# Mixture-of-experts weights on one core: all of the routed experts' low parts subtracted on VectorE, one buffer set for down's parts and the turned tokens, a third set of raw weights

## The chip, the cores and the metric

The kernel runs on one core of a Trainium2 chip. Time is device microseconds (us) of one execution, the median of a few runs. The engines of the core are named as the profile names them: PE (TensorE, matmuls; PEld is its weight load), DVE (VectorE), ACT (ScalarE), POOL (GpSimd) and SP (SyncE, which here issues most of the DMAs). TensorE's weight side is fed with a block of tokens, and the experts' weights stream past it.

## The reference

A decoder layer over 1024 tokens of width 1024: attention and an RWKV-7 recurrence side by side, then a mixture of experts. The change lies in the second half:

```
scores = sigmoid(h @ router_w)              # 64 experts in 8 groups
idx, wts = top 6 experts of a token, from its 4 best groups; wts normalised, times 2.5
routed  = sum over a token's 6 experts e of wts * (silu(h @ gate[e]) * (h @ up[e])) @ down[e]
shared  = (silu(h @ sh_gate) * (h @ sh_up)) @ sh_down
x = x + gate2 * (routed + shared);  out = rms_norm(x, final_g)
```

Every expert has gate and up of 1024 x 256 and down of 256 x 1024 float32, 1 MB each, so that the 64 experts hold 201 MB that each have to be read once.

## The kernel before

Products are made nearly as exact as float32 by splitting each operand into a high part (rounded to fp32r by a copy on ScalarE) and a low part (operand minus high part), and adding three products: high by high, high tokens by low weights, low tokens by high weights (`three`, line 1919). So the weights of each expert have to be split on the chip before TensorE may use them. One expert costs four pieces for gate and up (`split_gu`, line 1848: an ACT copy into `guh` on line 1853 and a DVE subtraction into `gul` on line 1854, each 128 x 1024) and two for down (`split_d`, line 1857: an ACT copy into `wdh` on line 1860 and a POOL subtraction into `wdl` on line 1861).

The router sorts the experts by their number of tokens into ranks. A table of fixed blocks (`BLOCKS`, line 1694) gives each rank its blocks of at most 128 token slots: 84 blocks for 64 experts, 20 experts with two to four blocks and 44 with one. Ranks of several blocks stand between those of one. Eight blocks of the shared expert come first. After about 1284 us of the profiled execution TensorE works on routed blocks alone.

`experts` (line 2018) is one loop over the blocks that is written out in full. All engines follow their instructions in the order written, so this order sets the schedule. In the round of block b stand, in this order:

- `up(b)`: 24 matmuls of 512 columns for gate and up;
- if block b is the first of its expert k (`turnover`, line 2053): three of the four pieces of `split_gu` for the next expert, k + 1;
- `act_t(b-1)`: two transposes of the activations, their high part `ah` (ACT, line 1942) and low part `al` (DVE, line 1944);
- `turn(b+1)`: eight transposes of the next block's gathered tokens `xg`, their high parts `xh` (ACT) and low parts `xl` (DVE, line 1915);
- `down(b-1)`: 12 matmuls into `yd`; every third pair (line 1923, `yd<-wdh,al`) needs `al`;
- `swiglu(b)` (ACT, DVE), then the fourth piece of `split_gu` and `split_d`, both for expert k + 1;
- `result(b-1)`: two DVE instructions `ye` (line 1956) and an indirect DMA from POOL that adds the rows to `d_acc` in DRAM (line 1958);
- at a turnover, `need_w(k+3)`: SP reads the expert's number and issues the DMAs of gate, up and down (`fetch`, line 1836). Also per block a gather of token rows `xg` three blocks ahead and of slots `sl` five blocks ahead, both issued by POOL.

Buffers: two sets of split weights (`sets`, for even and odd experts: gate and up and down, high and low), two raw buffers each of gate, up and down, two sets of turned tokens `xts`. A buffer's next user waits for the last user of its bytes, and nothing else.

Of the kernel before, what the change touches and what calls it, by code (L numbers as in the profile page):

```python
# [37 lines left out]
class Kern:  # L38
# [11 lines left out]
    # ---------------------------------------------------------------- constants  # L50
    def consts(self, ctx):
# [3 lines left out]
        with self.pool(name="cset", bufs=1) as sp, self.pool(name="csetp", bufs=1, space=PSUM) as pp:  # L55
# [60 lines left out]
            # silu of c, and the other derived columns  # L116
# [8 lines left out]
    def columns(self, pp):  # L125
        """the other parameters as columns"""
# [40 lines left out]
    # ---------------------------------------------------------------- DRAM scratch  # L167
# [53 lines left out]
    def ada(self, k):  # L221
        """a block of rows of the columns of shift1 and scale1"""
# [3 lines left out]
    def front(self, hp, load, first):  # L226
# [4 lines left out]
        with self.pool(name="frp", bufs=1, space=PSUM) as pp:  # L231
# [26 lines left out]
            def loads():  # L258
                """the rest of the adaLN columns, where x has been, and the first projection's"""
# [13 lines left out]
            def mods():  # L273
                """shift and scale: the sums over blocks of rows by VectorE, then those over lanes by TensorE"""
# [50 lines left out]
    # ---------------------------------------------------------------- projections, RWKV-7 and attention  # L325
    def phase_a(self, psum):
# [142 lines left out]
        # ---- features of RWKV-7  # L469
# [33 lines left out]
        def mixes():  # L503
            for j in range(15):
# [5 lines left out]
                if kind == "small":  # L510
# [3 lines left out]
                    # log_sigmoid and its running sum  # L514
# [76 lines left out]
        def sums(src):  # L591
            """of a pair's two heads, on all their partitions"""
# [4 lines left out]
        def rstds(w, pl, div, eps, least=None):  # L597
            """(sum / div + eps) ** -0.5 of a pair's two heads from the squares w, in rows of tokens and as wide as w"""
# [14 lines left out]
        def turned(w):  # L613
            """512 columns of them in the features' layout"""
# [7 lines left out]
        def kappa():  # L622
            """the scale of kappa"""
# [14 lines left out]
        def pre():  # L638
            """decay and learning rate"""
# [84 lines left out]
        def tokens(src, dst, p, h, pl, dup=None):  # L724
            """512 tokens of a pair's features -> rows of tokens in DRAM"""
# [59 lines left out]
        def merge():  # L785
            """the upper right block: Z11 X12 Z22"""
# [43 lines left out]
        # ---- the recurrence over chunks  # L830
# [10 lines left out]
        def feeds():  # L841
            """what the chain needs of every chunk: rows of v and the state, of b and k, and the inverse"""
# [24 lines left out]
        def prods():  # L867
            """masked products"""
# [82 lines left out]
        def ynorm():  # L951
            """(y - mean) * rstd of every head, in rows of tokens"""
# [22 lines left out]
        # ---- features of attention  # L975
# [4 lines left out]
        def parts(x, h, dst, p, hi, lo):  # L980
            """both parts of a pair's features to DRAM, by way of h: the leading ones from row hi of each head's, the others from row lo"""
# [85 lines left out]
        # ---- attention: the heads for the first half of the tokens, then for the second  # L1067
        def swap_fox():
# [9 lines left out]
            # leading parts of q (64 rows, two of ones, nothing, less the row's maximum) and of k (64 rows, less the running sum  # L1078
            # in two, nothing, ones), and both parts of q and, the other way round, of k
# [36 lines left out]
        def rowmax():  # L1116
            """the rows' maxima, of the scores' leading parts: they only keep exp in range, and cancel in the quotient"""
# [30 lines left out]
        def exps():  # L1148
            """exp of the turned scores, and the values"""
# [62 lines left out]
        # ---- the other adaLN rows, the output projection and the router  # L1212
# [55 lines left out]
    def weave(streams):  # L1268
        """Emits the steps of several (stream, lead) pairs in the order in which their engines would come to them;
        a stream with a lead is served earlier by so much.  # L1270
        A stream yields, after each step, what it held: (engine, time) pairs, ("DMA", latency), ("at", time),
        ("wait", key) and ("set", key) to follow other streams, ("lock", name) and ("unlock", name) to keep them out, ("~engine", time) for what the stream needn't wait for,
        and ("alloc", (name, buffers)) and ("free", name) around the use of shared buffers."""
# [3 lines left out]
        def take(s, t):  # L1277
            """runs one step of a stream and books its time"""
# [526 lines left out]
    def phase_b(self, pg, close_a4, h2):  # L1805
# [212 lines left out]
        def experts():  # L2018
# [13 lines left out]
            for b in range(NB + 1):  # L2032
# [51 lines left out]
                if b < NB:  # L2084
                    if b > 7:
                        need_t(b + 4)
# [97 lines left out]
```

## Time and profile before

| | us |
|---|---|
| three runs | 2237.56, 2241.24, 2254.24 (median 2241.24) |
| span of the profiled execution, first to last instruction | 2247.9 |
| routed blocks: first matmul of the first to last matmul of the last | 1284 to 2213 |
| weights of the first routed expert requested | 1254.9 |
| weights of the last one requested | 2176.9 (its down) |

For the profiled execution only its span is recorded. It is 6.7 us (0.3%) above the median of the runs, so a difference of time in the trace is set against the median as it stands.

How to read the profile: the page gives busy times and digits for 40 slices of 56.2 us, one digit a tenth, PEclk the granted TensorE clock, DMA the mean busy share of 16 DMA engines. The table of stretches gives the same for any window. A timeline row is start, duration, engine, line, operation, output<-inputs, shape, count, and in brackets how long the engine had been idle and what ended that. The table of waits adds those brackets up.

### The profile page before, as it was taken

To read this page: it belongs to the slowest core of one execution; us is meant where nothing else is said; L and a number is where in the kernel's file an instruction comes from. 1 tells how busy PE (TensorE), PEld (TensorE's weight loads), DVE (VectorE), ACT (ScalarE), POOL (GpSimd) and SP (SyncE) were. 2 spreads that over 40 slices of the span, in tenths; PEclk is the share of its full clock that TensorE was granted. 3 is DMA by queue.
4 is the path that set the end of the run, shared out by engine and by line. 5 is a ranking of instruction groups with operands and counts; after the bars stand their busy time and mean duration, and the time that the engine had idled before them with its cause. 6 is when DMAs were issued, how large, how long until landed. Compare 5 with 4: busy or idle time off the path is not lost. (4 is left out here: it accounts for less than half of the span.)

```text
span 2247.9 us, 28260 instructions
## 1 busy us (share of the span) xinstructions
PE 1916.8 (85%) x9746; PEld 1427.7 (64%) x9746; DVE 1489.7 (66%) x2453; ACT 919.3 (41%) x1402; POOL 1142.1 (51%) x830
## 2 busy tenths in 40 slices
PE   4898869889878888789898899888899999999993
PEld 3676657668666666546677677776666666666662
DVE  7736777583475566464777666777877777777774
ACT  5433433313222233343213344455555555555552
POOL 2222221222353233252466656767777777777773
PEclk7998987888878778789899999999999999999997
DMA  6124444646635277683744788899999999988875
GB/s 254 40 85 99 98 94 109 160 119 180 169 106 167 82 216 127 147 250 95 225 164 134 250 226 275 267 301 304 301 303 296 293 286 290 291 284 266 273 246 172
DMA packets 276770, 452.07 MB, mean 201 GB/s; under 512 B 132693, under 2 KB 202409, under 8 KB 250642
## 3 DMA queue, kind: packets, MB, share of 16 engines
q1 hardware_dynamic: 220578, 369.66, 51.3%
q0 software_dynamic: 24768, 66.75, 13.6%
q10 hardware_dynamic: 31280, 13.83, 2.3%
q8 instruction: 78, 1.28, 0.2%
q14 instruction: 66, 0.54, 0.1%
HBM read 355.27 MB, written 94.90 MB: 200 GB/s over the span
## 5 line engine op out<-in xcount | busy, mean ns | idle before, releaser
L1861 POOL TENSOR_TENSOR wdl<-down,wdh 128x1024 fp32r<-128x1024 f32 x128 | 341.0, 2664 | 124.7 <-ACT wdh L1860 124.4
L1854 DVE TENSOR_TENSOR gul<-gate,guh 128x1024 fp32r<-128x1024 f32 x128 | 295.1, 2306 | 62.3 <-ACT guh L1853 62.1
L366 POOL TENSOR_TENSOR wlo<-wraw,whi 128x1024 fp32r<-128x1024 f32 x30 | 78.5, 2617 | 360.4 <-ACT whi L364 340.6
L1958 POOL DMA_INDIRECT d_acc<-ye,ti x84 | 171.9, 2046 | 78.5 <-DVE gul L1854 23.9
L1923 PE MATMUL yd<-wdh,al 128*128 128x512 f32 (+6 forms) x368 | 130.1, 437 | 84.0 <-DVE al L1944 84.0
L1860 ACT ACTIVATE wdh<-down 128x1024 fp32r<-128x1024 f32 x128 | 128.6, 1052 | 173.3 <-issue 172.6
L1923 PE MATMUL gu<-guh,xh 128*128 128x512 f32 (+6 forms) x736 | 192.6, 405 | 1.6 <-ACT xh L1914 1.6
L1923 PE MATMUL gu<-guh,xl 128*128 128x512 f32 (+6 forms) x736 | 185.8, 394 | 0.1
L1923 PE MATMUL gu<-gul,xh 128*128 128x512 f32 (+6 forms) x736 | 185.3, 394 | 0.0
L1923 PEld LDWEIGHTS gu<-guh,xh 128*128 128x128 f32 (+6 forms) x736 | 129.5, 176 | 54.6 <-issue 5.0
L1854 DVE TENSOR_TENSOR gul<-up,guh 128x1024 fp32r<-128x1024 f32 x128 | 158.1, 1235 | 5.6 <-ACT guh L1853 5.0
L1923 PEld LDWEIGHTS gu<-guh,xl 128*128 128x128 f32 (+6 forms) x736 | 121.9, 166 | 49.2 <-issue 1.0
L1923 PEld LDWEIGHTS gu<-gul,xh 128*128 128x128 f32 (+6 forms) x736 | 122.0, 166 | 47.7
L439 PE MATMUL zp<-hTl,whi 128*128 128x512 f32 x480 | 146.9, 446 | 0.0
L1942 ACT ACTIVATE ah<-g 128x256 fp32r<-128x256 f32 (+5 forms) x92 | 31.3, 340 | 280.1 <-PE g L1940 266.9
L439 PE MATMUL zp<-hTh,wlo 128*128 128x512 f32 x480 | 143.7, 437 | 0.0
L1923 PEld LDWEIGHTS yd<-wdh,al 128*128 128x128 f32 (+6 forms) x368 | 63.5, 182 | 125.0 <-DVE al L1944 104.0
L1853 ACT ACTIVATE guh<-gate 128x1024 fp32r<-128x1024 f32 x128 | 134.0, 1047 | 8.1 <-DMA gate<-in_exp_w_gate_dram 8.1
L1956 DVE SCALAR_TENSOR_TENSOR ye<-yd,sl,g 128x512 f32<-128x512 f32 (+12 forms) x168 | 120.6, 740 | 24.8 <-PE yd L1923 21.4
L439 PE MATMUL zp<-hTh,whi 128*128 128x512 f32 x480 | 136.6, 424 | 0.0
L1853 ACT ACTIVATE guh<-up 128x1024 fp32r<-128x1024 f32 x128 | 134.8, 1053 | 2.0 <-DMA up<-in_exp_w_up_dram 2.0
L1923 PE MATMUL yd<-wdh,ah 128*128 128x512 f32 (+6 forms) x368 | 128.8, 433 | 4.2 <-ACT ah L1942 3.7
(461 smaller groups left out, 4238.3 us busy)
## 6 DMA issues: line engine op xcount, KB each, us to landing
gate<-in_exp_w_gate_dram SPq DMA_DIRECT2D x64, 1024.0 KB
up<-in_exp_w_up_dram SPq DMA_DIRECT2D x64, 1024.0 KB
down<-in_exp_w_down_dram SPq DMA_DIRECT2D x64, 1024.0 KB
mw<-in_ada_w_dram SPq DMA_DIRECT2D x32, 512.0 KB
wraw<-in_w_in_dram SPq DMA_DIRECT2D x30, 512.0 KB
xw<-in_ada_w_dram SPq DMA_DIRECT2D x8, 1024.0 KB
xw<-in_x_dram SPq DMA_DIRECT2D x8, 512.0 KB
fb<-d_fb SPq DMA_DIRECT2D x16, 256.0 KB
```

Source lines behind the costliest of these rows:

```text
L366: (nc.vector if j == 1 else nc.gpsimd).tensor_sub(lo, w, h.bitcast(F32))
L439: nc.tensor.matmul(z, a[:, d, :], b[:, d, hs], start=(n == 0 and d == 0), stop=(n == 2 and d == 7))
L1853: nc.scalar.activation(gh[:, qs, n, :], t[:, qs], AF.Copy)
L1854: nc.vector.tensor_sub(gl[:, qs, n, :], t[:, qs], gh[:, qs, n, :].bitcast(F32))
L1860: nc.scalar.activation(dh[:, j], raw[2][:, j], AF.Copy)
L1861: nc.gpsimd.tensor_sub(dl[:, j], raw[2][:, j], dh[:, j].bitcast(F32))
L1923: nc.tensor.matmul(z, x[:, d, :], w[:, d, cs], start=(m == 0), stop=(m == 3 * n - 1))
L1942: nc.scalar.activation(ah[:, :, 0:n], tp[:, :, 0:n], AF.Copy)
L1956: nc.vector.scalar_tensor_tensor(y[0:n, hs], zs[h][0:n], wt, B["g2"][0:n, hs], op0=OP.mult, op1=OP.mult)
L1958: nc.gpsimd.indirect_dma_start(out=self.d_acc, out_offset=ind(ti), in_=y[0:n], in_offset=None, compute_op=OP.add)
```

## The change

- `split_d` subtracts on DVE instead of POOL. In the routed experts POOL then only issues DMAs. (The shared expert's six pieces, `shared`, are unchanged, three of them still on POOL.)
- Down's parts have one buffer set, `wds`, for all experts instead of one in each of two. `split_d` for expert k therefore no longer stands in the round of the first block of k - 1, but at the end of the round of the first block of k, behind `result(b-1)`; its ACT copies wait until `down(b-1)`, the last use by expert k - 1, is through.
- Turned tokens have one set, `xts`, instead of two.
- Raw weights have three buffers each instead of two. `need_w(k+4)` now requests gate and up of expert k + 4 and down of expert k + 3, in two calls of `fetch`, each with a read of the expert's number of its own. Before the loop three experts are requested (of the third gate and up alone).
- The costs with which the order is planned while the first blocks share the engines with the routing are adapted.

Lines in the changed kernel are 1 to 5 higher (1854 becomes 1857, 1861 becomes 1864, 1944 becomes 1947). The diff, without comment lines and without changed signatures that follow from it:

```
         def weight_set(wp):
-            return [wp.tile([128, 8, 2, FE], F32R, name=f"gu{n}") for n in "hl"] + [
-                wp.tile([128, 2, D], F32R, name=f"wd{n}") for n in "hl"]
+            return [wp.tile([128, 8, 2, FE], F32R, name=f"gu{n}") for n in "hl"]
...
-            sets.append(weight_set(pool("bw0")))
+            wp = pool("bw0")
+            sets.append(weight_set(wp))
+            wds.extend(wp.tile([128, 2, D], F32R, name=f"wd{n}") for n in "hl")
...
-            xts.extend([B["fp"].tile([128, 8, 128], F32R, name=f"x{k}{i}", bufs=1) for k in "hl"] for i in range(2))
+            xts.extend(B["fp"].tile([128, 8, 128], F32R, name=f"x{k}", bufs=1) for k in "hl")
...
-            for n, j, c in (("gate", 8, FE), ("up", 8, FE), ("down", 2, D)):
-                t = B["wp"].tile([128, j, c], F32, name=n, bufs=2)
+            for n, j, c in which:
+                t = B["wp"].tile([128, j, c], F32, name=n, bufs=3)
...
+        GU, DN = (("gate", 8, FE), ("up", 8, FE)), (("down", 2, D),)
...
-        def split_d(raw, k):
-            dh, dl = sets[k % 2][2:]
+        def split_d(raw):
+            dh, dl = wds
             for j in range(2):
-                nc.scalar.activation(dh[:, j], raw[2][:, j], AF.Copy)
-                nc.gpsimd.tensor_sub(dl[:, j], raw[2][:, j], dh[:, j].bitcast(F32))
+                nc.scalar.activation(dh[:, j], raw[0][:, j], AF.Copy)
+                nc.vector.tensor_sub(dl[:, j], raw[0][:, j], dh[:, j].bitcast(F32))
                 yield
...
         def need_w(k):
-            if k < NK:
-                raws[k] = fetch(self.eid[0:1, order[k]:order[k] + 1])
+            for kk, to, which in ((k, raws, GU), (k - 1, rawd, DN)):
+                if 0 < kk < NK:
+                    to[kk] = fetch(self.eid[0:1, order[kk]:order[kk] + 1], which)
...
-            need_w(1)
-            need_w(2)
+            for k in range(1, 4):
+                need_w(k)
...
                 if b < NB:
                     act = swiglu(z, m), m
-                    if turnover:
-                        work.append(split_d(raws[k + 1], k + 1))
-                    pieces(2)
+                    pieces(99)
...
                 if b > 0:
                     result(zs, blocks[b - 1][2], weight_of(b - 1), tis[b - 1])
...
-                pieces(99)
                 if b < NB:
+                    if k and blocks[b - 1][0] != k:
+                        work.append(split_d(rawd[k]))
+                        pieces(99)
                     if b > 7:
                         need_t(b + 4)
                     if turnover:
-                        need_w(k + 3)
+                        need_w(k + 4)
```

How this moves instructions, at three places. First VectorE, in the round of a block that is the first of its expert (`gul` gate and up, `al` the activations, `xl` the tokens, `act` the product in SwiGLU, `ye` the result, `ti` the token numbers of a later block). Before:

```order
L1854 TENSOR_TENSOR gul<-gate,guh 128x4x256
L1854 TENSOR_TENSOR gul<-up,guh 128x4x256
L1854 TENSOR_TENSOR gul<-gate,guh 128x4x256
L1944 TENSOR_TENSOR al<-g,ah 128x256
L1915 TENSOR_TENSOR xl_9133<-tp,xh_9132 128x512 x2
L1934 TENSOR_TENSOR act<-act,gu 128x256
L1854 TENSOR_TENSOR gul<-up,guh 128x4x256
L1956 SCALAR_TENSOR_TENSOR ye<-yd,sl,g_8180 128x512 x2
L1893 CAST ti<-sl 128x1
```

And now:

```order
L1857 TENSOR_TENSOR gul<-gate,guh 128x4x256
L1857 TENSOR_TENSOR gul<-up,guh 128x4x256
L1857 TENSOR_TENSOR gul<-gate,guh 128x4x256
L1947 TENSOR_TENSOR al<-g,ah 128x256
L1918 TENSOR_TENSOR xl<-tp,xh 128x512 x2
L1937 TENSOR_TENSOR act<-act,gu 128x256
L1857 TENSOR_TENSOR gul<-up,guh 128x4x256
L1959 SCALAR_TENSOR_TENSOR ye<-yd,sl,g_8180 128x512 x2
L1864 TENSOR_TENSOR wdl<-down,wdh 128x1024 x2
L1896 CAST ti<-sl 128x1
```

Two subtractions of down have come in behind `ye`, and so ahead of the next round's `gul` and `al`; nothing else has changed places. Second GpSimd, two rounds of first blocks before, and three now:

```order
L1888 DMA sl<-d_slot,d_sidx_9830 96x2
L1861 TENSOR_TENSOR wdl<-down,wdh 128x1024
L1958 DMA d_acc<-ye,ti 1152x1024
L1861 TENSOR_TENSOR wdl<-down,wdh 128x1024
L1898 DMA xg<-d_h_191,ti 96x1024
L1888 DMA sl<-d_slot,d_sidx_9830 128x2
L1861 TENSOR_TENSOR wdl<-down,wdh 128x1024
```

```order
L1901 DMA xg<-d_h_191,ti 64x1024
L1891 DMA sl<-d_slot,d_sidx_9826 64x2
L1961 DMA d_acc<-ye,ti 1152x1024
L1901 DMA xg<-d_h_191,ti 64x1024
L1891 DMA sl<-d_slot,d_sidx_9826 128x2
L1961 DMA d_acc<-ye,ti 1152x1024
L1901 DMA xg<-d_h_191,ti 64x1024
```

The subtractions on both sides of the scatter-add are gone, and three DMA issues a block are left. Third SyncE, the requests of one turnover and the start of the next, before:

```order
L1838 TENSOR_LOAD d_eid
L1838 ISA x2
L1842 ISA
L1842 DMA gate<-in_exp_w_gate_dram 128x2048
L1842 ISA
L1842 DMA up<-in_exp_w_up_dram 128x2048
L1842 ISA
L1842 DMA down<-in_exp_w_down_dram 128x2048
L1838 TENSOR_LOAD d_eid
```

And now:

```order
L1839 TENSOR_LOAD d_eid
L1839 ISA x2
L1843 ISA
L1843 DMA gate<-in_exp_w_gate_dram 128x2048
L1843 ISA
L1843 DMA up<-in_exp_w_up_dram 128x2048
L1839 TENSOR_LOAD d_eid
L1839 ISA x2
L1843 ISA
L1843 DMA down<-in_exp_w_down_dram 128x2048
L1839 TENSOR_LOAD d_eid
```

The down that is requested is now that of the expert before, and its number is read once more. ScalarE's rows keep their order (`wdh` twice behind the fourth `guh` in both), but the two `wdh` now belong to the block's own expert instead of the next.

More of the change, by code (lines that the diff above doesn't have):

```diff
@@ L1845, in fetch @@
             return res
+        GU, DN = (("gate", 8, FE), ("up", 8, FE)), (("down", 2, D),)
         def split_gu(raw, k):
-            gh, gl = sets[k % 2][:2]
+            gh, gl = sets[k % 2]
             for q in range(2):
                 qs = slice(q * 4, q * 4 + 4)
-                for n, t in enumerate(raw[:2]):
+                for n, t in enumerate(raw):
                     nc.scalar.activation(gh[:, qs, n, :], t[:, qs], AF.Copy)
@@ L1899, in rows, with turn @@
             return x
-        def turn(b, x, n, turned=False):
-            xh, xl = xts[b % 2]
+        def turn(x, n, turned=False):
+            xh, xl = xts
             if turned:
@@ L1928, in up @@
             z = B["z"] = B["pp"].tile([128, 512], F32, name="gu")
-            return three(z[0:n], xt, [t.rearrange("p j n f -> p j (n f)") for t in w[:2]], 8, slice(None))
+            return three(z[0:n], xt, [t.rearrange("p j n f -> p j (n f)") for t in w], 8, slice(None))
         def swiglu(z, n):
@@ L1945, in act_t, with down @@
             return ah[:, :, 0:n], al[:, :, 0:n]
-        def down(a, w, n):
+        def down(a, n):
             zs = B["zs"] = [B["pp"].tile([128, 512], F32, name="yd") for _ in range(2)]
             for h in range(2):
-                yield from three(zs[h][0:n], a, w[2:], 2, slice(h * 512, (h + 1) * 512))
+                yield from three(zs[h][0:n], a, wds, 2, slice(h * 512, (h + 1) * 512))
         def result(zs, n, wt, ti):
@@ L2052, in experts @@
                         need_s(b + 5)
-                    turnover = k + 1 < NK and (blocks[b - 1][0] != k if k else b == 6)
-                    if turnover:
+                    turnover = k + 1 < NK + 1 and (blocks[b - 1][0] != k if k else b == 6)
+                    if turnover and k + 1 < NK:
                         work.append(split_gu(raws[k + 1], k + 1))
@@ L2063, in experts @@
                 if b + 1 < NB:
-                    xt = turn(b + 1, xs[b + 1], blocks[b + 1][2], b < 7)
+                    xt = turn(xs[b + 1], blocks[b + 1][2], b < 7)
                     if b < 8:
@@ L2067, in experts @@
                 if act is not None:
-                    for s in down(at, sets[blocks[b - 1][0] % 2], act[1]):
+                    for s in down(at, act[1]):
                         if b < 8:
@@ L2073, in experts @@
                     act = swiglu(z, m), m
-                    if turnover:
-                        work.append(split_d(raws[k + 1], k + 1))
-                    pieces(2)
+                    pieces(99)
                     if b < 8:
@@ L2087, in experts @@
                     if turnover:
-                        need_w(k + 3)
+                        need_w(k + 4)
                     if turnover and b < 8:
-                        yield [("~ACT", 4.0), ("~DVE", 2.8), ("~POOL", 4.6)]
+                        yield [("~ACT", 2.0), ("~DVE", 2.3), ("~POOL", 1.0)]
         def rest():
@@ L2099, in rest @@
                 nc.vector.tensor_copy(ei[:, 1:2], self.os[:, ds(o, 1)])
-                raw = fetch(ei[0:1, 0:1])
+                raw, rawd = fetch(ei[0:1, 0:1], GU), fetch(ei[0:1, 0:1], DN)
                 sl = slots(ei[:, 1:2], 128)
@@ L2103, in rest @@
                 x = rows(ti, 128)
-                g, h = split_gu(raw, 0), split_d(raw, 0)
-                xt = turn(0, x, 128)
+                g, h = split_gu(raw, 0), split_d(rawd)
+                xt = turn(x, 128)
                 for s in (g, h):
@@ L2111, in rest @@
                 at = act_t(swiglu(B["z"], 128), 128)
-                for _ in down(at, sets[0], 128):
+                for _ in down(at, 128):
                     pass
```

10 lines of the change are left out of this document (5 added, 5 removed).

## The prediction

> **What bounds the kernel now.** I began with the page: its slices show where each resource is full.
>
> ```profile
> PE   4898869889878888789898899888899999999993
> POOL 2222221222353233252466656767777777777773
> PEclk7998987888878778789899999999999999999997
> DMA  6124444646635277683744788899999999988875
> ...
> L1861 POOL TENSOR_TENSOR wdl<-down,wdh 128x1024 fp32r<-128x1024 f32 x128 | 341.0, 2664 | 124.7 <-ACT wdh L1860 124.4
> L1854 DVE TENSOR_TENSOR gul<-gate,guh 128x1024 fp32r<-128x1024 f32 x128 | 295.1, 2306 | 62.3 <-ACT guh L1853 62.1
> ...
> L1854 DVE TENSOR_TENSOR gul<-up,guh 128x1024 fp32r<-128x1024 f32 x128 | 158.1, 1235 | 5.6 <-ACT guh L1853 5.0
> ```
>
> From slice 24 on (the routed experts) both PE and DMA stand at 8 to 9 tenths. And one thing is odd: the same subtraction costs 2306 ns for gate and 1235 for up. Next, the table of stretches, from the first routed blocks to where the last weights have landed, with 20 us of a full queue ahead of them:
>
> ```profile
> core 0: us, PE busy (x) PEld busy (x) DVE busy (x) ACT busy (x) POOL busy (x), PEclk, DMA share, GB/s
> 1262.00:1282.00 20.00, 18.28 (x81) 14.91 (x81) 10.51 (x18) 7.60 (x11) 13.01 (x8) 0.95 1.02 388
> 1275.00:1400.00 125.00, 117.78 (x551) 95.05 (x550) 77.31 (x107) 54.16 (x84) 77.43 (x47) 0.97 0.86 261
> 1400.00:1500.00 100.00, 87.36 (x403) 69.17 (x402) 77.70 (x88) 54.40 (x77) 74.85 (x40) 0.96 0.87 278
> 1500.00:1800.00 300.00, 272.19 (x1244) 201.76 (x1243) 228.89 (x276) 163.20 (x234) 224.01 (x125) 0.96 0.96 300
> 1800.00:2000.00 200.00, 180.16 (x828) 122.99 (x825) 156.15 (x183) 112.95 (x163) 159.49 (x83) 0.97 0.91 287
> 2000.00:2182.00 182.00, 165.95 (x757) 111.76 (x758) 132.29 (x170) 95.51 (x141) 140.76 (x75) 0.97 0.86 277
> ```
>
> From 1275 to 2182 are 907 us. PE is busy for 823.4 of them (117.78 + 87.36 + 272.19 + 180.16 + 165.95), idle for 83.6. The clock column loses 3 to 4% more: 31 us. The DMA engines' work, share by length, is 107.5 + 87 + 288 + 182 + 156.5 = 821 us: almost as much as PE's. What ends PE's idle time, and what SP's requests wait for, stands in the two tables of waits for the same stretch:
>
> ```profile
> PE yd L1923 <- DVE al L1944: 82.3, 42, 4.7
> ...
> SPq L1842 <- POOL wdl L1861: 479.5, 62, 8.8
> SPq L1842 <- DVE gul L1854: 273.1, 73, 23.7
> ```
>
> So nearly all of PE's idle time is one wait: `down` stops at its third pair for `al`, 42 times at 2.0 us. And the next weights are requested when POOL or DVE lets a raw buffer go; SP waits for that 750 us. Last, the timeline of one round that splits weights:
>
> ```profile
> 1714.46 2.01 ACT L1860 ACTIVATE wdh<-down 128x1024 fp32r<-128x1024 f32 x2 [2.16 <-issue]
> 1716.38 1.04 ACT L1853 ACTIVATE guh<-gate 128x1024 fp32r<-128x1024 f32 x1
> ...
> 1715.60 2.40 POOL L1861 TENSOR_TENSOR wdl<-down,wdh 128x1024 fp32r<-128x1024 f32 x1 [1.37 <-ACT wdh L1860]
> 1718.17 2.26 POOL L1958 DMA_INDIRECT d_acc<-ye,ti  x1 [0.16 <-issue]
> 1719.97 2.88 POOL L1861 TENSOR_TENSOR wdl<-down,wdh 128x1024 fp32r<-128x1024 f32 x1
> 1723.01 1.74 POOL L1898 DMA_INDIRECT xg<-d_h,ti  x1 [0.16 <-issue]
> ...
> 1712.38 1.27 DVE L1915 TENSOR_TENSOR xl<-tp,xh 128x512 fp32r<-128x512 f32 x2
> ...
> 1713.58 0.40 DVE L1934 TENSOR_TENSOR act<-act,gu 96x256 f32<-96x256 f32 x1
> ...
> 1715.04 1.40 DVE L1956 SCALAR_TENSOR_TENSOR ye<-yd,sl,g 96x512 f32<-96x512 f32 x2
> 1716.36 0.14 DVE L1893 CAST ti<-sl 96x1 int32<-96x1 f32 x1
> 1717.45 1.64 DVE L1854 TENSOR_TENSOR gul<-gate,guh 128x1024 fp32r<-128x1024 f32 x1 [0.95 <-ACT guh L1853]
> 1719.01 1.21 DVE L1854 TENSOR_TENSOR gul<-up,guh 128x1024 fp32r<-128x1024 f32 x1
> 1720.15 3.79 DVE L1854 TENSOR_TENSOR gul<-gate,guh 128x1024 fp32r<-128x1024 f32 x1
> 1723.86 0.34 DVE L1944 TENSOR_TENSOR al<-g,ah 128x192 fp32r<-128x192 f32 x1
> ...
> 1714.44 2.03 PE L1923 MATMUL gu<-guh,xh 128*128 128x512 f32 x8
> ...
> 1724.26 0.70 PE L1923 MATMUL yd<-wdh,al 128*96 128x512 f32 x2 [1.73 <-DVE al L1944]
> ...
> 1726.19 2.01 PE L1923 MATMUL gu<-guh,xh 128*72 128x512 f32 x8
> ```
>
> Here is the odd thing's cause. POOL's second subtraction holds from 1719.97 to 1722.85; DVE's `gul`, issued at 1720.15, ends 1.09 later, at 1723.94. The 1.64 beside POOL's first one ends 1.09 after that as well. The two engines' subtractions take turns. `al` stands behind them, PE waits 1.73, and the round takes 11.75 (1714.44 to 1726.19). Undisturbed rows, and a round that splits nothing:
>
> ```profile
> 1958.01 1.22 DVE L1854 TENSOR_TENSOR gul<-gate,guh 128x1024 fp32r<-128x1024 f32 x1
> 1958.45 2.25 POOL L1958 DMA_INDIRECT d_acc<-ye,ti  x1 [1.19 <-DVE ti L1893]
> 1959.14 1.22 DVE L1854 TENSOR_TENSOR gul<-up,guh 128x1024 fp32r<-128x1024 f32 x1
> 1960.28 1.22 DVE L1854 TENSOR_TENSOR gul<-gate,guh 128x1024 fp32r<-128x1024 f32 x1
> ...
> 1957.08 2.00 PE L1923 MATMUL gu<-guh,xh 128*72 128x512 f32 x8
> ...
> 1966.73 0.63 PE L1923 MATMUL gu<-guh,xh 128*72 128x512 f32 x2
> ```
>
> A subtraction costs DVE 1.14 from start to start, also beside a scatter-add issued by POOL. A round without a stall takes PE 9.65.
>
> **The change, part by part.** *Down's low part on DVE.* It takes 2664 ns off POOL 128 times and gives DVE 1.14 instead; and `gul` loses its waits. A round that splits then costs DVE six subtractions, 6.84, `al` 0.34, `act` 0.40, `ye` 1.40, `ti` 0.14 and the tokens' two `xl`, 1.27 for 128 tokens: 10.4. Before, it was 1.64 + 1.21 + 3.79 + 1.21 for `gul` alone, and 11.4 in all. A round that splits nothing costs DVE 3.55. For 64 and 20 of them: 666 + 71 = 737, against PE's 84 x 9.65 = 811: DVE isn't the bound on average.
>
> *Where the stall goes.* Laid out with the rows of the round at 1714: `wdh` 1714.46 to 1716.47, `ye` to 1716.36, then `wdl` twice to 1718.64, `gul` three times to 1722.06. `al` starts there instead of at 1723.86, and PE is ready for it at 1722.53 (1724.26 - 1.73). The stall is gone with 0.4 to spare. What is late next: rounds that split come about three in a row (64 in 84). Each takes DVE 0.75 more than PE's 9.65, so the stalls are about 0, 0.35 and 0.75 there, and 0.75 more with a fourth; a round without splitting clears the debt. With 20 groups that leaves 22 to 37 us. PE's limit from 1284 to 2213 is then 811 + 22 to 37 against 929 now: a gain of 81 to 96. The half-clock stretches, which follow the stalls, are in it.
>
> *Transfers.* They must go 8% faster for that, and have 821 us of work in 907. The most that the trace shows over 300 us is 0.96, with requests still waiting for buffers; with a full queue it is 1.02 (first row of the table). A third raw buffer keeps three experts requested. I take 0.98, in between: 821 / 0.98 = 838, and 4 us more since the first 125 us, with four blocks on one expert, cannot be filled entirely: 842, a gain of 65. At 1.02 it would be 98, at 0.95 39. At 0.98 it is smaller than PE's, so the transfers decide, and the third buffer is worth what lies between 0.96 (859, a gain of 48) and 0.98: about 17 us (none, if 0.96 is the most; 50 at 1.02).
>
> *One buffer set for down.* `wdh` now waits for the `down` just ahead of it. But it did so before: at 1714.46 it began together with the next `up` (1714.44), as `down` ended, since the set of two experts back was in use until then too. ACT's order is the same. The cost is nothing as long as `wdl` is through before the next `down` asks for it, a pair of matmuls before `al`, at about 1722; it is through at 1718.64. PE's `up` and transposes are the cover. Without them copies and subtractions would cost 1718.64 - 1714.46 = 4.2 us a turnover, 267 in all.
>
> *One set of turned tokens.* `xh` waits for the previous `up`; it waited for transposes that stand behind that `up` on PE anyway. Only in the eight shared blocks, which aren't transposed, is it new; there `ah`, ahead of it on ACT, waits for PE's transposes behind `up` too. Nothing; without that cover one `xh` and `xl`, some 2 us, seven times.
>
> *SP's second read of the expert's number.* 64 more; SP waits for buffers 750 of 907 us. Nothing.
>
> The sum: 65 us off 2241, the profiled span being 6.7 over the median: **2176 us**.
>
> **Rivals.**
> *Transfers give way.* If 0.96 is a queue that waits, and not work, PE's limit decides: 81 to 96 off, 2152. For it speaks the 388 GB/s row; against it that 300 GB/s was held for 300 us while requests were outstanding. The Trainium skill (DMA: Bandwidth & Descriptors, Bandwidth) gives HBM about 358 GB/s for a core; the 258 MB that the table's rows add up to would then need an estimated 721 us, and PE would decide. The trace's 388 GB/s over 20 us is above that figure, so I don't sum with it.
>
> *VectorE takes the stall over.* If small gaps between instructions add 0.4 to each round, DVE's 10.4 becomes 10.8, and if the slack of the plain rounds isn't used (`al` is needed in each round, and split weights can be only one expert ahead), a splitting round takes 11.0 to 11.5: 64 x 11.0 to 11.5 + 20 x 9.65 = 897 to 929 against 929, 0 to 32 off: 2225 in the middle. For it: six subtractions in a row now stand ahead of `al`. Against: the laid-out round above has 0.4 to spare.
>
> *Slower: GpSimd's DMA issues take turns with the subtractions* as its own subtractions did. With `d_acc` (2.26) and `xg` (1.74) a block on DVE's bill, DVE needs 737 + 84 x 4.0 = 1073 for 929: 144 slower, 2385. It decides from 2.3 us a block on. Against it: `gul` took 1.22 beside `d_acc` at 1958.45. The Trainium skill (SBUF — State Buffer, Who interferes with whom) says that a VectorE instruction with two SBUF inputs contends with a GpSimd one that reads SBUF, not with one that only writes; the 3.79 and the 1.22 agree.
>
> **How the numbers follow.** Transfers decide, 2176: 0.70, its own range 2143 to 2202 (shares of 1.02 to 0.95). They give way: 0.10. VectorE takes over: 0.13. Slower: 0.07. For 8 in 10 the range takes the first two and most of the third's near side: 2143 to 2216. A measurement tells about 1% (22 us) from no change. Faster by more: 0.70 + 0.10 + a quarter of the third, 0.84; the rest of the third, 0.09, is within 1%; slower 0.07.
>
> **What would show it.** Right: `gul` of gate near 1.22 like up's; PE's waits for `al` under 40 us in all; DMA share 0.97 or more from 1400 to 2050; now and then ACT's `guh` or `wdh` waiting for a landing. Wrong: `gul` or `wdl` over 1.5 (the slower rival); DVE over 0.95 busy with PE still waiting for `al` (VectorE); shares of 0.9 with neither PE nor DVE full, which none of this explains.

## The result, and the profile after

| | before | after |
|---|---|---|
| median of the runs, us | 2247.74 (2237.56 to 2263.71, 4 runs) | 2180.41 (2171.78 to 2194.53, 4 runs) |
| ratio of the times, 95% interval | | 0.9713 (0.9634 to 0.9792) |
| profiled execution: span, us | 2247.9 | 2192.3 (its own time: 2194.53) |
| routed blocks, first matmul to last, us | 1284.2 to 2213.1 = 928.9 | 1298.3 to 2158.8 = 860.5 |

The change saves 67 us where 65 were predicted (2176, range 2143 to 2216). The routed part became 68.4 us shorter. The profiled execution came to that part 14 us later than before. The experiments below, the one with the old front too, came there between 1280 and 1304, so I take this for scatter; it is part of why this execution lies above the median.

The page of the changed kernel, the same lines as before, and the gathers of slots:

```profile
PE   4898888898887789798978889999899998999993
POOL 3322222313433314325256744654556666776652
PEclk7999686888878777799989989999999999999996
DMA  7124354555455365966365498999999999999875
...
L1891 POOL DMA_INDIRECT sl<-d_slot,d_sidx x84 | 198.6, 2364 | 27.5 <-issue 24.4
...
L1857 DVE TENSOR_TENSOR gul<-up,guh 128x1024 fp32r<-128x1024 f32 x128 | 155.5, 1215 | 5.5 <-ACT guh L1856 5.2
...
L1857 DVE TENSOR_TENSOR gul<-gate,guh 128x1024 fp32r<-128x1024 f32 x128 | 155.3, 1214 | 0.0
...
L1864 DVE TENSOR_TENSOR wdl<-down,wdh 128x1024 fp32r<-128x1024 f32 x128 | 150.0, 1210 | 0.1
```

All three kinds of subtraction now take the same 1.21 us; gate's came down from 2306 ns. GpSimd lost 341 us of subtractions, but it is busy for only 169 us less (972.9 after 1142.1), mostly because its DMA issues became longer: `sl` has a mean of 2364 ns, and had 1147 before (102 us more in all), and `xg` takes 31 us more. The stretches of the routed part:

```profile
1275.00:1400.00 125.00, 123.24 (x573) 100.14 (x574) 85.13 (x127) 55.01 (x83) 56.47 (x38) 0.98 0.92 305
1400.00:1500.00 100.00, 97.78 (x465) 76.82 (x463) 83.08 (x114) 60.17 (x85) 61.22 (x29) 1.00 0.96 310
1500.00:1800.00 300.00, 275.52 (x1282) 202.19 (x1282) 237.16 (x331) 173.36 (x247) 175.63 (x85) 0.98 0.96 311
1800.00:2000.00 200.00, 192.67 (x917) 132.19 (x916) 165.44 (x235) 119.55 (x176) 135.28 (x62) 1.00 0.95 316
2000.00:2115.00 115.00, 114.28 (x546) 79.12 (x545) 100.09 (x144) 72.12 (x107) 81.46 (x36) 1.00 0.95 318
```

The last three columns say most: the clock hardly falls any more (stretches at half the clock cost 8.5 us of the routed part, and 32.4 before, worked out from the trace), and the transfers run at 305 to 318 GB/s where they ran at 261 to 300, at a share that is no higher from 1500 to 1800 (0.96) and 0.04 to 0.09 higher elsewhere. TensorE is nearly full in all rows but the third, from 1500 to 1800. What the engines waited for from 1275 to 2160:

```profile
DVE ti L1896 <- DMA sl<-d_slot,d_sidx: 56.3, 34, 4.3
...
DVE ye L1959 <- DMA d_acc<-ye,ti: 41.0, 18, 5.6
...
PE yd L1926 <- DVE al L1947: 25.1, 23, 2.4
...
PE tp L1915 <- DMA xg<-d_h,ti: 10.4, 9, 2.1
```

TensorE's wait for `al` fell from 82.3 to 25.1. Three waits are new (of `xg` there was one before, 1.2), and all three are for GpSimd's small transfers (slots, sums, tokens). None is for weights. Last, the timeline of VectorE and GpSimd in a round that splits weights:

```profile
1575.17 1.40 DVE L1959 SCALAR_TENSOR_TENSOR ye<-yd,sl,g 88x512 f32<-88x512 f32 x2
...
1576.42 6.77 POOL L1891 DMA_INDIRECT sl<-d_slot,d_sidx  x1 [0.30 <-issue]
1576.49 2.35 DVE L1864 TENSOR_TENSOR wdl<-down,wdh 128x1024 fp32r<-128x1024 f32 x2
...
1578.83 1.20 DVE L1857 TENSOR_TENSOR gul<-gate,guh 128x1024 fp32r<-128x1024 f32 x1
...
1579.96 1.21 DVE L1857 TENSOR_TENSOR gul<-up,guh 128x1024 fp32r<-128x1024 f32 x1
...
1581.09 1.21 DVE L1857 TENSOR_TENSOR gul<-gate,guh 128x1024 fp32r<-128x1024 f32 x1
...
1582.58 0.38 DVE L1947 TENSOR_TENSOR al<-g,ah 128x216 fp32r<-128x216 f32 x1 [0.28 <-ACT ah L1945]
```

This is the round that the prediction laid out: `ye`, `wdl` twice, `gul` three times, then `al`, which here waits for `ah` and not for a subtraction. Beside it GpSimd's gather, issued at 1576.42, holds until 1583.19, past the whole run of subtractions, which themselves take their 1.21 (2.35 for two, 1.14 from start to start).

### The profile page after: what moved, and what is told of

It is laid out like the page before. It is cut to its first block, busy times and chain, and to the rows that moved or that the text cites. A ratio compares the mean times of both kernels' runs of the same rounds, so it can differ in the third digit from the quotient of the medians.

```text
span 2192.3 us, 28289 instructions
## 1 busy us (share of the span) xinstructions
PE 1903.1 (87%) x9746; PEld 1417.6 (65%) x9746; DVE 1494.5 (68%) x2581; ACT 918.9 (42%) x1402; POOL 972.9 (44%) x702
## 5 line engine op out<-in xcount | busy, mean ns | idle before, releaser
L1961 POOL DMA_INDIRECT d_acc<-ye,ti x84 | 176.9, 2106 | 282.2 <-issue 65.1
L1891 POOL DMA_INDIRECT sl<-d_slot,d_sidx x84 | 198.6, 2364 | 27.5 <-issue 24.4
L1863 ACT ACTIVATE wdh<-down 128x1024 fp32r<-128x1024 f32 x128 | 128.6, 1052 | 95.6 <-PE yd L1926 91.9
L1901 POOL DMA_INDIRECT xg<-d_h,ti x84 | 150.3, 1789 | 25.8 <-issue 20.9
L1926 PEld LDWEIGHTS gu<-guh,xh 128*128 128x128 f32 (+6 forms) x736 | 125.0, 170 | 50.8 <-ACT xh L1917 1.8
L1857 DVE TENSOR_TENSOR gul<-gate,guh 128x1024 fp32r<-128x1024 f32 x128 | 155.3, 1214 | 0.0
L1864 DVE TENSOR_TENSOR wdl<-down,wdh 128x1024 fp32r<-128x1024 f32 x128 | 150.0, 1210 | 0.1
L1926 PE MATMUL yd<-wdh,al 128*128 128x512 f32 (+6 forms) x368 | 121.2, 411 | 25.6 <-DVE al L1947 25.1
```

Of the source, the lines that this page charges most:

```text
L1857: nc.vector.tensor_sub(gl[:, qs, n, :], t[:, qs], gh[:, qs, n, :].bitcast(F32))
L1863: nc.scalar.activation(dh[:, j], raw[0][:, j], AF.Copy)
L1864: nc.vector.tensor_sub(dl[:, j], raw[0][:, j], dh[:, j].bitcast(F32))
L1891: nc.gpsimd.indirect_dma_start(out=sl[0:n], out_offset=None, in_=self.d_slot, in_offset=ind(idx[0:n]))
L1901: nc.gpsimd.indirect_dma_start(out=x[0:n], out_offset=None, in_=self.d_h2, in_offset=ind(ti))
L1926: nc.tensor.matmul(z, x[:, d, :], w[:, d, cs], start=(m == 0), stop=(m == 3 * n - 1))
```

## The experiments

Theory A is the prediction's: the two engines' subtractions took turns, and with that gone transfers set the first half of the routed part and TensorE the second. Theory B has the gain in the earlier requests of the third raw set, Theory C says that GpSimd's late DMAs cost what is still waited for. D to I come up with the later experiments and are told in their expectations.

The first four share one set of runs of the kernel before (2243.22 us), the next four a second (2245.99), then three (2247.62) and one (2249.57).

**Where the gain is from: e1_dve_only.** The kernel before with this edit alone (two raw sets, two sets of down's parts and of turned tokens):

```
-                nc.gpsimd.tensor_sub(dl[:, j], raw[2][:, j], dh[:, j].bitcast(F32))
+                nc.vector.tensor_sub(dl[:, j], raw[2][:, j], dh[:, j].bitcast(F32))
```

> The kernel before, with one instruction moved: down's low part is subtracted on VectorE, at the old place, with two sets of split weights, two of turned tokens and two raw buffers. Theory A (the gain comes from the subtractions of two engines no longer taking turns): most of the 67 us, so 2180 to 2205, and gate's `gul` at about 1.22 us like up's. Theory B (the gain comes from earlier requests, by the third raw set): 2225 to 2250, within 1% of before.

Measured: 2189.51 us, 0.9758 (0.9698 to 0.9818): 54 us of the gain, by the moved subtraction alone, in Theory A's range; Theory B falls. The 9 us to the changed kernel are within the two intervals.

**The third raw set: e2_two_raw.** The changed kernel with two raw sets:

```
-                t = B["wp"].tile([128, j, c], F32, name=n, bufs=3)
+                t = B["wp"].tile([128, j, c], F32, name=n, bufs=2)
...
-            for k in range(1, 4):
+            for k in range(1, 3):
...
-                        need_w(k + 4)
+                        need_w(k + 3)
```

> The changed kernel with two raw buffers instead of three (requests one expert later). Theory A: 0 to 20 us slower than the changed kernel, 2180 to 2200; by the prediction's estimate 17. Theory B: at least half of the gain is lost, 2215 or more.

Measured: 2182.04 us, 0.9733 (0.9664 to 0.9802). The third set is worth nothing that can be measured.

**Taking turns: e3_pool_again.** The changed kernel with the old place of down's subtraction:

```
-                nc.vector.tensor_sub(dl[:, j], raw[0][:, j], dh[:, j].bitcast(F32))
+                nc.gpsimd.tensor_sub(dl[:, j], raw[0][:, j], dh[:, j].bitcast(F32))
```

> The changed kernel with down's low part back on GpSimd; one set of down's parts, one of turned tokens and three raw sets stay. Theory A: no faster than before, 2240 to 2340, since POOL's two subtractions of 2.7 us now begin only when down of the expert before is through, and hold up the three `gul` and `al` behind them; gate's `gul` back at 2.3 us or more on average. Theory B: 2180 to 2205.

Measured: 2400.85 us, 1.0703 (1.0636 to 1.0770), 220 us over the changed kernel, and above Theory A's range too. Its groups of subtractions, from the page:

```profile
L1857 DVE TENSOR_TENSOR gul<-gate,guh 128x1024 fp32r<-128x1024 f32 x128 | 373.5, 2918 | 76.9 <-ACT guh L1856 76.9
L1864 POOL TENSOR_TENSOR wdl<-down,wdh 128x1024 fp32r<-128x1024 f32 x128 | 337.5, 2926 | 0.0
```

Gate's is lengthened from 1214 to 2918 ns by nothing but the other engine's subtraction; GpSimd's own takes 2926, and took 2664 in the kernel before. So the lengthening is the place of `wdl`, as the prediction read it, and neither buffers nor order cure it. It is worse than the kernel before by 158 us. In the new order `wdl` stands right ahead of the next round's `gul`; that more of them meet there fits the 2918 against 2306, but was not tried by itself.

**The late slots: e4_slots_early.** After the change VectorE waits 56.3 us for slots. Here they are gathered seven blocks ahead:

```
-            sl = B["fp"].tile([128, 2], F32, name="sl", bufs=8)
+            sl = B["fp"].tile([128, 2], F32, name="sl", bufs=12)
...
-                        need_s(b + 5)
+                        need_s(b + 7)
```

> The changed kernel with the slots' gathers issued two rounds earlier (seven blocks ahead instead of five, 12 buffers instead of 8), so that the token numbers on VectorE find them landed. Theory C (what is left of TensorE's waits comes from GpSimd's DMA issues, which in the changed kernel's trace take up to 6.8 us behind a run of subtractions, so that `ti` waits 56 us): 10 to 30 us faster than the changed kernel, 2150 to 2170, and `ti` waits under 10 us. Theory A (the transfers decide in the first half of the blocks and TensorE in the second): within 10 us of the changed kernel, with the same DMA share of 0.95 or 0.96 from 1500 to 1760.

Measured: 2177.94 us, 0.9710 (0.9651 to 0.9769): no change, though `ti` no longer waits; Theory C falls. Its waits show the next one in line:

```profile
DVE ye L1959 <- DMA d_acc<-ye,ti: 65.3, 26, 7.6
```

This was 41.0: the wait moved from the slots to the sums. A table of VectorE's waits alone would have promised 56 us.

**Do transfers decide: e5_half_down and e6_more_loads.** Both are e2 with other loads, in `fetch`; half of down (both halves of its split then read the half that is loaded):

```
+                src = A["exp_w_" + n][0][ds(e, 1)].rearrange("e r c -> (e r) c").rearrange("(p j) c -> p j c", j=j)
+                o = 1 if n == "down" else j
+                nc.sync.dma_start(t[:, 0:o], src[:, 0:o])
```

and half of gate once more, which nothing reads:

```
+                if n == "up":
+                    g = B["wp"].tile([128, 4, FE], F32, name="more", bufs=2)
+                    nc.sync.dma_start(g, A["exp_w_gate"][0][ds(e, 1)].rearrange("e r c -> (e r) c").rearrange(
+                        "(p j) c -> p j c", j=j)[:, 0:4])
```

> The kernel with two raw sets (e2_two_raw, 2182 us) in which only the first half of each expert's down weights is loaded, and both halves of the subtraction read it; it leaves out half of down's weights, 64 x 0.52 MB = 33.5 MB, which at the 311 GB/s of the stretch 1500 to 1800 and its share 0.96 is an estimated 103 us of transfer time at a full share. Theory D (transfers set the pace while 24 of the 90 routed rounds take 10.9 us each, and TensorE's own 9.7 us a round sets it afterwards): the rounds of blocks 28 to 52 fall from 256-262 us to TensorE's 233 to 240, blocks 8 to 28 gain up to 10, and the rest nothing, so 2145 to 2165 us. Theory E (VectorE's queue and GpSimd's held DMA issues set the pace of these rounds as well, and the share of 0.97 is only what they leave): unchanged within 10 us, 2172 to 2192.

> The kernel with two raw sets (2182 us) with an additional load of 0.52 MB an expert into a tile that nothing reads, 33.5 MB in all, an estimated 103 us of transfer time at the rate of the stretch 1500 to 1800. Theory D: the rounds that transfers already set (about 24 of 90) take their whole share of it, some 27 us, and the later ones, which had 3 to 10% of the transfer engines' time left, most of the rest: 2225 to 2275 us, with a DMA share near 0.97 to the end of the routed part. Theory E: the DMA engines have room, and the time rises by less than 15 us, 2172 to 2197.

Measured: e5 2159.08 us, 0.9634 (0.9566 to 0.9702), 23 less than e2 (the intervals overlap a little, at 0.966 to 0.970; the routed parts are 840.1 and 853.6); e6 2221.55 us, 0.9897 (0.9813 to 0.9982), 40 more (routed part 891.2). Theory E falls: loads set part of the time. But 103 us of transfers were worth only 23 and 40, and e6 is under Theory D's range. Its stretches tell why:

```profile
1500.00:1800.00 300.00, 261.36 (x1192) 190.39 (x1192) 222.12 (x307) 157.60 (x226) 154.79 (x80) 0.96 1.00 332
1800.00:2000.00 200.00, 186.58 (x866) 127.95 (x865) 158.00 (x223) 115.52 (x168) 118.37 (x56) 0.97 0.98 332
2000.00:2115.00 115.00, 114.23 (x541) 77.98 (x540) 96.35 (x138) 69.56 (x102) 76.83 (x36) 1.00 1.03 359
```

The same engines carry 332 to 359 GB/s when more is asked of them, where 311 went at a share of 0.96. So 0.96 was no ceiling. Nor is a packet's time fixed: in the queue of SP's loads a MB took the 16 engines 2.78 us before, 2.71 after and in e6 (1500 to 1800), and 2.61 in e6 from 2000 to 2115 (that queue's share times the length, over its MB).

How transfers then decide is in the chain of waits from 1500 to 2100 (shares of these 600 us; "d_acc" is the scatter-add, until it has landed). With half of down:

```profile
by line: PE gu L1927 32.7%; PE yd L1927 17.4%; DMA d_acc<-ye,ti 15.4%; issue 8.9%; PE tp L1916 5.8%; DMA sl<-d_slot,d_sidx 4.8%; DMA xg<-d_h,ti 4.3%; DVE gul L1858 3.4%; POOL sl L1892 2.8%; PE g L1944 1.1%; DVE ye L1960 0.6%; DVE xl L1919 0
```

With more loads:

```profile
by line: DMA d_acc<-ye,ti 33.1%; issue 15.4%; PE gu L1930 13.1%; DMA sl<-d_slot,d_sidx 11.1%; PE yd L1930 8.6%; DVE gul L1861 6.5%; POOL sl L1895 2.8%; PE tp L1919 2.0%; POOL xg L1905 1.5%; DVE ye L1963 1.4%; DVE wdl L1868 1.1%; DVE xl L192
```

With fewer loads the chain runs through TensorE's matmuls (33 + 17%), with more through the small transfers (33 + 11%). The weights come in time either way (with more loads ACT waits 3.1 us for them in all); the small transfers beside them come late.

**The order on VectorE: e7_two_pieces and e9_four_pieces.** The changed kernel with one piece of the split less, or more, at the head of a round:

```
-                    pieces(3)
+                    pieces(2)
```

> The changed kernel with two pieces of the weight split at the head of a round instead of three: the third of the 1.21 us subtractions then stands behind VectorE's copies for the running block, so that al comes about 1.2 us earlier on VectorE and the run of subtractions ahead of it, in which GpSimd's DMA issues are held up to 6.77 us, is shorter. Theory E: TensorE's waits for al (25.1 us) go and held issues get shorter, so 5 to 20 us less than the changed kernel, 2160 to 2175. Theory D: the waits for al fall too, but the time stays within 8 us of the changed kernel's 2180.

Measured: 2210.15 us, 0.9854 (0.9784 to 0.9925): 30 slower than the changed kernel. In the profiled executions 17 us of it lie in the routed part (877.5 after 860.5); the rest is not explained here. Both theories missed it, and the reason for the experiment was wrong in itself: `al` did come sooner, but what waited instead was this (TensorE, 1300 to 2160):

```profile
PE tp L1915 <- DMA xg<-d_h,ti: 31.0, 11, 5.7
PE yd L1926 <- DVE al L1947: 11.9, 19, 1.4
```

The subtraction taken from ahead of `al` now stands ahead of `ye`. The scatter-add needs `ye`, and later blocks' gathers stand behind the scatter-add in GpSimd's queue. The reverse, `pieces(4)`, was to test that:

> The reverse of e7_two_pieces: all four pieces of the next expert's split stand at the head of the round, so that four 1.21 us subtractions run ahead of al, and nothing but act stands between al and ye. Theory F (what the order decides is when ye is ready, since GpSimd's scatter-add waits for it, and the gathers of later blocks stand behind that scatter-add in GpSimd's queue; e7 put a subtraction ahead of ye and lost 30 us): ye comes earlier, so the time is that of the changed kernel or up to 15 us less, 2165 to 2182, although al comes 1.2 us later. Theory E (the run of subtractions ahead of al, in which GpSimd is held, decides): a longer run, so 10 to 30 us more, 2190 to 2210, with more of TensorE's waits for al and more than 40 DMA issues of over 2.9 us.

Measured: 2188.91 us, 0.9766 (0.9698 to 0.9834), 8.5 over the changed kernel: within the intervals, and between the two theories' ranges. The held issues are gone, which Theory E had not expected at all (GpSimd, 1300 to 2115):

```profile
L1901 POOL DMA_INDIRECT xg<-d_h,ti x80 | 98.6, 1233 | 26.3 <-issue 21.8 <-PE yd L1926 3.0 <-PE tp L1915 0.9
L1891 POOL DMA_INDIRECT sl<-d_slot,d_sidx x79 | 85.9, 1087 | 24.1 <-issue 24.1
```

`sl` is at 1087 ns again, 8 issues of all take over 2.9 us where 40 did, and TensorE waits 2.3 us for `xg`. Yet no time is won: `al`, behind four subtractions, made TensorE wait 38.1 us in place of 25.1. So taking the held issues away did not pay for 13 us more of that wait; what they cost by themselves is not shown. That e7 lost its time by the late `ye` fits the 31.0, and e9's 2.3 on the other side; the link by link chain was not shown.

**What holds an issue: e10_memset.** Behind each subtraction an instruction that reads nothing:

```
+                    nc.vector.memset(gap, 0.0)
```

> The changed kernel with a VectorE memset of one column (which reads nothing) behind every fp32 subtraction of the weights: 6 an expert, an estimated 0.06 to 0.1 us each, 0.4 to 0.6 us a round on VectorE. Theory G (a DMA issue of GpSimd is held while VectorE runs instructions with both operands in SBUF back to back, and goes on at the first instruction of another kind): the issues of over 2.9 us (40 in the changed kernel) nearly vanish, and the mean sl issue falls from 2.4 us to under 1.6; if such issues also cost time, 5 to 15 us are won less the memsets, 2168 to 2185. Rival (the issue is held by something else, the semaphores or the queue): sl's issues stay above 2 us, and the time rises by the memsets, 2180 to 2200.

Measured: 2184.39 us, 0.9731 (0.9671 to 0.9792); 35 issues over 2.9 us, `sl` 2.24 us in the mean. Theory G falls, the rival's forecast holds. A gather in this kernel:

```profile
1568.61 6.57 POOL L1895 DMA_INDIRECT sl<-d_slot,d_sidx  x1 [0.30 <-issue]
...
1573.08 1.21 DVE L1858 TENSOR_TENSOR gul<-gate,guh 128x1024 fp32r<-128x1024 f32 x1
1573.09 0.06 DVE L1859 MEMSET gap<- 128x1 f32 x1
...
1574.22 0.37 DVE L1951 TENSOR_TENSOR al<-g,ah 128x216 fp32r<-128x216 f32 x1
```

It ends at 1575.18, 0.96 after `al`, which reads PSUM, begins; 0.99 is the median of a `sl` issue. So it made next to no way during the subtractions, and 0.06 us of another kind between them do not help. Whether they are too short, or run within the neighbour's time, stays open. In the changed kernel's 40 issues of over 2.9 us, the time with no weight subtraction beside them is 0.92 us in the median, worked out from the trace: about a plain gather's time.

But not every issue is held. The changed kernel's trace also has this gather, with the same neighbours as the one at 1576.42:

```profile
1520.47 1.02 POOL L1891 DMA_INDIRECT sl<-d_slot,d_sidx  x1 [0.30 <-issue]
...
1520.54 2.35 DVE L1864 TENSOR_TENSOR wdl<-down,wdh 128x1024 fp32r<-128x1024 f32 x2
```

Of 57 issues that began in a run of subtractions (or at most 0.2 us ahead of it) with 2 us or more of it to come, 32 lasted past its end and 25 ended inside it. In the kernel before, 51 scatter-adds of 54 ended inside. What tells the two kinds apart is not shown.

**More room for the small transfers: e8_room and e11_room_slots.** The changed kernel with two raw sets, slots 7 blocks ahead, tokens 4 ahead in 6 buffers, token numbers a block sooner, 4 buffers for `ye`:

```
-            x = B["fp"].tile([128, D], F32, name="xg", bufs=4)
+            x = B["fp"].tile([128, D], F32, name="xg", bufs=6)
...
-            y = B["fp"].tile([128, D], F32, name="ye")
+            y = B["fp"].tile([128, D], F32, name="ye", bufs=4)
...
-                        need_s(b + 5)
+                        need_s(b + 7)
...
-                        need_t(b + 4)
+                        need_t(b + 5)
```

> A candidate for a better version: the changed kernel with two raw sets, whose room goes to the running gathers and sums: slots gathered 7 blocks ahead (12 buffers), tokens 4 ahead (6 buffers), turned tokens one block earlier, 4 buffers for ye. It takes out all the waits for late GpSimd transfers at once (ti for sl, PE for xg, ye for d_acc), which together ended 108 us of idle time on three engines. Theory E: 10 to 25 us less than the changed kernel, 2155 to 2170. Theory D: those waits move to the weights' landings, which come no earlier, and the time stays within 10 us, 2170 to 2190.

Measured: 2209.38 us, 0.9849 (0.9779 to 0.9919), 29 slower than the changed kernel and outside both theories' ranges; in the profiled executions 15 us of it lie in the routed part (875.2). VectorE's first wait names a buffer that I had not enlarged, that of `ti`:

```profile
DVE ti L1896 <- DMA d_acc<-ye,ti: 75.4, 23, 8.4
```

`ti` cannot be written before the scatter-adds that read its old contents are done. With 12 buffers for it (`name="ti", bufs=12`):

> e8_room with 12 buffers for ti in place of 8. In e8 ti, needed one block earlier, waited 75.4 us for the scatter-adds that still read its 8 buffers, which delayed al (TensorE's waits 42.2 us). Theory H (that wait is all that cost e8 its 29 us over the changed kernel): ti no longer waits, and the time falls to 2160 to 2185. Rival (more gathers ahead are late or harmful for another reason, for example because ye then runs further ahead of its scatter-adds or the gathers take the place of scatter-adds in GpSimd's queue): it stays above 2195.

Measured: 2196.25 us, 0.9796 (0.9739 to 0.9853). 13 of the 29 us are back, a difference within the intervals, and the time is just inside the rival's range (above 2195). In the profiled execution the routed part is 861.7, as long as the changed kernel's 860.5, but this execution, 2186.45, is the shortest of its four. This fits that wait being the routed part's loss, but single executions do not show it, and the rest of the 29 is open. No version here beats the changed kernel.

**Is TensorE the limit: e12_two_terms.** A third of `up` left out in the routed blocks:

```
-                    for s in up(xt, sets[k % 2], m):
+                    for s in up(xt, sets[k % 2], m, 3 if b < 8 else 2):
```

> The changed kernel in which the routed blocks leave out the third of up's three terms (the low part of the tokens times the high part of the weights): 8 of 36 matmuls, about 2.0 us of TensorE's 9.7 us a round; VectorE's work, the loads and the order stay. Theory D (transfers set blocks 28 to 52, TensorE the blocks after): blocks 28 to 52 stay at 255 to 262 us; the others fall until the transfers set them too, which at a share of 0.98 is 809 us in place of 844 for blocks 8 to 91, so at most 35 us less: 2145 to 2170, with a DMA share of 0.96 or more in the last third. Theory I (TensorE's own work sets the pace everywhere, and a share of 0.97 is no limit): 2.0 us less in each of 83 rounds, 166 us, so below 2100. Theory E (the order of VectorE and GpSimd sets it): no change within 10 us, with the DMA share as it was.

Measured: 2168.75 us, 0.9637 (0.9559 to 0.9716): 12 us less than the changed kernel, which its interval does not tell from nothing, for 166 us of TensorE's work. Theory I falls, and Theory E's 10 us are missed by 2. Theory D's range holds, but not its reason, as the time of the routed blocks shows (from first matmul to first matmul, with the DMA share, worked out from the trace; the last weights land before the last stretch ends; the last row is the prediction's 9.65 a round):

| us (share) | blocks 8 to 28 | 28 to 52 | 52 to 72 | 72 to 91 |
|---|---|---|---|---|
| before | 219 (0.86) | 266 (0.96) | 221 (0.92) | 210 (0.81) |
| changed | 196 (0.93) | 263 (0.97) | 201 (0.95) | 185 (0.86) |
| e2, two raw sets | 198 (0.91) | 256 (0.97) | 199 (0.96) | 186 (0.91) |
| e5, fewer loads | 195 (0.87) | 248 (0.93) | 199 (0.92) | 184 (0.83) |
| e6, more loads | 198 (0.94) | 277 (1.00) | 217 (0.98) | 185 (0.99) |
| e12, fewer matmuls | 195 (0.94) | 255 (0.98) | 203 (0.96) | 181 (0.87) |
| TensorE's own 9.65 | 193 | 232 | 193 | 183 |

The changed kernel's first and last stretch run at TensorE's own pace. But with 2 us a round taken from TensorE they keep their time. So another limit lies within a few us of TensorE's there. The trace points at VectorE in the rounds that split: from first matmul to first matmul, e12's take 10.0 us in the first stretch and 9.6 in the last, and VectorE is busy for 9.1 and 9.0 of them. In e12 TensorE waits for `al` again, and VectorE for small transfers (1275 to 2140):

```profile
PE yd L1926 <- DVE al L1947: 92.8, 56, 3.8
...
DVE ti L1896 <- DMA sl<-d_slot,d_sidx: 67.1, 33, 5.7
```

In the middle the loads move the time (248 to 277 in blocks 28 to 52, 199 to 217 in 52 to 72, the latter only upwards), and the matmuls hardly do (255 and 203, beside e2's 256 and 199).

## Why the prediction was right, and where it wasn't

- *Subtractions of two engines take turns.* Shown: gate's `gul` 2306 to 1214 ns, and 2918 with `wdl` back on GpSimd (e3). The prices of 1.14 from start to start and 1.22 for one held for `wdl` too.
- *The stall at `al` goes, and 22 to 37 us come back in runs of split rounds.* TensorE waited 25.1 for `al`, and 10.4 more for `xg`, which the prediction had not named. The table of blocks has 16 experts of several blocks and 48 of one (not 20 and 44, as the description of the kernel has it), so the split rounds come in 16 groups of mostly four, not in 20, and the prediction's own prices give 0.35 + 0.75 + 0.75 for each, 30 in all. In the routed part TensorE's idle time fell by 46.5 us (84.75 to 38.22) and its busy time for the same matmuls by 21.5 (844.25 to 822.78), as the granted clock rose from 0.97 to 0.99: together the 68.
- *Transfers decide, at 821 us of work and a share of 0.98.* The sum 842 was near the 833 measured (1289 to 2122), by two errors against each other; that the whole came out within 2 us is luck. The share from 1400 to 2050 was 0.96, not 0.97 and more. And the work was less than 821: with the 14 us of later start, from 1289 to 2122, the shares add up to an estimated 788 (0.91 x 111 + 0.96 x 400 + 0.94 x 322), for the same 258 MB. The failed step is that a share times its length was taken as work that stays. The rival "transfers give way" had this part right; e6 showed it, at 332 to 359 GB/s. That transfers decide holds for the middle blocks alone (28 to 72); at both ends loads hardly move the time.
- *A third raw buffer is worth about 17 us.* It is worth nothing that can be measured (e2), so this term of the sum was mis-sized. SP's requests still waited for buffers afterwards (667 us, 1275 to 2160), so the prediction's sign that buffers were short was no sign that weights came late: ACT's copies waited for a landing 8.4 and 2.0 us in the whole run, as before (8.1 and 2.0). The prediction's "now and then" did not happen.
- *One buffer set for down and for the turned tokens costs nothing.* Nothing that can be measured: e1 has both sets and isn't faster. ACT's `wdh` waits 91.9 us for `yd`, hidden as laid out.
- *The slower rival, GpSimd's issues against subtractions.* They do contend, but the other way round: `gul` and `wdl` keep 1.21, the issue often waits, up to 6.77 us. The prediction's row, `gul` 1.22 beside `d_acc`, showed only the side that doesn't suffer. What the waiting costs is not shown by itself: e9 had 8 held issues in place of 40 and won nothing, with more waiting for `al`. The Trainium skill (SBUF — State Buffer, Who interferes with whom) infers that such a subtraction doesn't stop descriptors from being made, because it takes only the read side of the shared ports, and making descriptors needs the write side. The 6.77 and e10's 6.57 disagree with that for these indirect DMAs, though 25 of the 57 above ended inside a run; the turns of the two subtractions, which both read SBUF, agree with its taking the read side.
- *VectorE takes the stall over.* Not in the changed kernel, where it is busy for 0.68 to 0.87 of a row, but it, with the waits in its queue, is the nearest candidate for what e12 ran into. Whether VectorE's own work or the late small transfers in its queue set those rounds stays open; no kernel with less work on VectorE was tried.

## What to carry to other kernels

When one instruction has two prices in one profile (1235 and 2306), look for the other engine's instruction that it ends with: moving one of the two so that both stand on one engine saved 54 us, although VectorE got more to do. A busy share of the DMA engines is not work, and requests that wait for a buffer are no shortage: ask whether a reader ever waited for the landing. Before paying for a wait in a table of waits, see what stands next in line; here waits of 56, 41 and 10 us could be taken away (slots in e4, sums in e11, tokens in e9), and the time stayed or rose.

## What the hardware showed unexpectedly

- A GpSimd DMA issue of about 1 us can be held through an unbroken run of VectorE subtractions whose operands both lie in SBUF (6.77 us at most in the changed kernel), and e10's moved on when one that reads PSUM ran. It happened to 32 of 57 issues; the others got through, and what decides is open. The subtractions aren't lengthened (1.20 to 1.22 us).
- The DMA engines carried 311 GB/s at a share of 0.96 (after), and 332 at 0.98 to 1.00 and 359 at 1.03 with 33.5 MB more to load (e6), which cost 40 us in place of 103.
- With TensorE's holes gone, its clock was granted at 0.98 to 1.00 from 1275 to 2115, where it was 0.96 to 0.97; the same matmuls were busy 21.5 us less, of the 68 in the routed part. In e12, whose TensorE idles for 130 us of its routed part, the clock is 0.93 there.
